# Renewing the normalized input ahead of the value projection, and second parts of every other weight unit by an adding transfer

## The chip, the core and the metric

The kernel runs on one core of a Trainium2 chip. The metric is the device time of one execution in microseconds (us), the median of several. TensorE (PE) does the matrix products, VectorE (DVE) and ScalarE (ACT) the elementwise work, GpSimd (POOL) a few small operations and a part of the transfers, and SyncE (SP) issues the others.

## What is computed

The reference is a trunk of two layers over 512 tokens of width 1024. A layer normalizes its input, projects it, runs three mixers beside each other (a recurrence, A; latent attention, B; forgetting attention, C), merges them with sigmoid gates that are made from the same normalized input, and then runs a feed-forward part and a per-layer input part.

```
for i in range(DEPTH):                        # DEPTH = 2
    h = rmsnorm(x, mix_norm[i])
    z = h @ w_in[i]
    u_rnn, u_gelu, c_q, ckv_rope, fq, fk, fv, f_logit, gate_logit = split_columns(z)
    y_a = rglru_branch(u_rnn, u_gelu, ...) @ w_br_a[i]      # conv, gates, scan over the tokens
    y_b = mla_branch(c_q, ckv_rope, ...) @ w_br_b[i]
    y_c = fox_branch(fq, fk, fv, f_logit, ...) @ w_br_c[i]  # softmax, causal, forget bias
    g = sigmoid(gate_logit + gate_b[i])                     # three gates of width 1024
    merged = g[0] * y_a + g[1] * y_b + g[2] * y_c
    x = x + merged @ w_o[i]
    x = x + swiglu(rmsnorm(x, ffn_norm[i]))
    x = x + sigmoid(rmsnorm(x, ple_norm[i]) @ w_ple_gate[i]) * (p[i] @ w_ple[i])
return rmsnorm(x, final_norm)
```

## The kernel before

Every activation lies as pages of 128 channels x 512 tokens, eight pages for width 1024. To keep float32 accuracy each factor of a product is held in two parts: a high part, rounded by a cast, and a low part, which is the value less its high part. One 128x128 tile of weights times one page is then three matmuls of 128x512 (`mm3`): high by high, high by low, low by high. A page of two parts lies in the pool `pr` (31 pages), a plain page in `pf` (20 pages).

The weights are one stream of 606 units of 128x512 (four 128x128 tiles each, so twelve matmuls a unit), in the order in which the program uses them. SP loads a unit into one of 4 buffers `raw`. `Stream._split` makes the parts: ACT casts the high part (L112) and DVE subtracts it from the loaded unit (L113), into one of 8 buffers `hl`. A unit's buffer comes free when the last of its matmuls has run, and then the unit that comes eight later can be split into it.

In a layer's mixing stage (`mix`) the first projections use pages `X`, which are x times the gain without the division by the norm, since the norm isn't known yet; each result is multiplied by the row of reciprocal norms `r` afterwards (`scaled`, one DVE instruction each, 128x512). Later projections use `Xn`, the input normalized in full. `renorm` makes page k of it: a DMA in POOL's queue loads x again from DRAM (L695, from `xT` in layer 0 and from the scratch `xs` in layer 1) into a `pf` page, DVE multiplies by gain and `r` (a scalar_tensor_tensor with `vec`), ACT casts the high part, DVE subtracts for the low part. `drop_x` gives the pages `X` and `r` back.

The order in question is this. After the gates of the recurrence come `lru_tail` (ACT square roots; then for each of four channel groups a multiply-add, a product, a scan over the tokens at L666, a product with the GELU branch, and the split into `yA`), the value projection of mixer C (`values`, units 24 to 31 in layer 0), and then `attention`, which sets score and probability products among a plan of other projections: key projection 1 (`fp(1, 0)`, units 32 and 33), the merge of channel group 0 (`mg(0, 0)`, its gate of units 34 and 35, and its product with `yA`), the gate of group 1 (`mg(0, 1)`), query projection 1 (`fp(1, 1)`) and so on. In the kernel before, the first three of these use `X` and `r`; the eight renewals stand in the plan between them, in three portions, and `fp(1, 1)` is the first to need `Xn`. No line orders engines directly: a scheduler lists the instructions of each engine from the program's order, its priorities (the splitting of weights has a high one) and its own estimates, and that list then stands.

Of the kernel before, what the change touches and what calls it, by code (L numbers as in the profile page):

```python
# [10 lines left out]
F32 = mybir.dt.float32  # L11
F32R = mybir.dt.float32r
I32 = mybir.dt.int32
AF = mybir.ActivationFunctionType
ALU = mybir.AluOpType
# [3 lines left out]
KD = D // 128  # L19
# [18 lines left out]

NUNITS = 606
KEPT = NUNITS - 16  # L40
PACKED = (8, 9, 311, 312)


# [41 lines left out]
class Stream:  # L85
# [15 lines left out]
    def _split(self, u):  # L101
        s = (u % self.nraw) * 512
        src = self.raw[:, s:s + 512]
        if u >= KEPT:
            self.kept[u] = self.pages.take()
        hi, lo = self._parts(u)
        if u in PACKED:
            hi, lo = (x.rearrange("p (k c) -> p k c", c=128)[:, :, 64 * i:64 * i + 64]
                      for i, x in ((0, hi), (1, hi)))
            src = src.rearrange("p (k c) -> p k c", c=128)[:, :, 0:64]  # L110
        with self.tc.high_priority():
            self.nc.scalar.copy(hi, src)  # L112
            self.nc.vector.tensor_tensor(lo, src, hi.bitcast(F32), op=ALU.subtract)  # L113

    def _parts(self, u, c=slice(0, 512)):
        if u in self.kept:
# [5 lines left out]
    def _ensure(self, u):  # L122
        last = min(u + self.nhl - 1, max(u + 4, KEPT - 1), NUNITS - 1)
        while self.loaded < min(self.nraw, NUNITS):
            self._load(self.loaded)
            self.loaded += 1
        while self.done <= last:
            self._split(self.done)
            self.done += 1
            while self.loaded < min(self.done + self.nraw, NUNITS):  # L130
                self._load(self.loaded)
                self.loaded += 1
# [34 lines left out]
class Trunk:  # L167
# [273 lines left out]
    def mix(self, layer):  # L441
        nc = self.nc
        L, st, X = layer, self.st, self.xp
# [42 lines left out]
        rT = self.cols(NT)  # L486
# [24 lines left out]
        def key_and_forget():  # L511
# [3 lines left out]
            for k, x in enumerate(X):  # L515
                assert self.w.pos // 4 in PACKED
                wh, _ = self.w.tile(("kf", L, k))
# [84 lines left out]
        def fox_proj(p, X, r):  # L602
            return [
                self.dense(self.win(L, C_FK + 128 * p), X, ev_heads(kp, p, r, True, False)),
                self.dense(self.win(L, C_FQ + 128 * p), X, ev_heads(qp, p, r, True, True)),
            ]

        def values(spec, X, rT):

            V = []  # L610
            bs = [self.banks.take() for _ in range(NT)]
            for k, x in enumerate(X):
                wh, wl = self.w.wide(spec + (k,))
                for j in range(NT):
                    c = slice(j * 128, (j + 1) * 128)
                    self.mm3(bs[j][:, :], x.h[:, c], x.l[:, c], wh, wl, k == 0, k == len(X) - 1)
                    yield
            for j in range(NT):
                g = pr.take()
                V.append(g)  # L620
                dst = g.ap.rearrange("p (h t d) -> p h t d", h=HEADS, t=2)
                src = bs[j].rearrange("p (h d) -> p h d", h=HEADS)
                hi = dst[:, :, 0, :]
                if rT is None:
                    self.split(hi, dst[:, :, 1, :], src)
                else:
                    r = rT[:, j:j + 1]
                    self.act(hi, src, AF.Copy, scale=r)
                    self.stt(dst[:, :, 1, :], src, r, hi.bitcast(F32), ALU.mult, ALU.subtract)
                self.banks.give(bs[j])  # L630
            self.V = V


        yA = [None] * 4
# [20 lines left out]
        def lru_tail():  # L655

            with ExitStack() as after:
                for i in last_tanh:
                    after.enter_context(self.tc.issue_after(i.ins))
                for q in tT:  # L660
                    self.act(q.ap, q.ap, AF.Sqrt, bias=self.eps[:, 1:2])
            for t in range(4):
                a, bb, q = aT[t], bT[t], tT[t]
                self.stt(q.ap, a.ap, 1.0, q.ap, ALU.add, ALU.mult)
                self.tt(bb.ap, bb.ap, q.ap)
                nc.vector.tensor_tensor_scan(q.ap, a.ap, bb.ap, 0.0, op0=ALU.mult, op1=ALU.add)  # L666
                self.stt(q.ap, q.ap, 0.25, gx[t].ap, ALU.mult, ALU.mult)
                yA[t] = pr.take()
                self.split(yA[t].h, yA[t].l, q.ap)
                for p in (q, a, bb, gx[t]):  # L670
                    p.free()
# [13 lines left out]
            p.free()  # L685

        lru_tail()
        self.run(values(("fv", L), X, rT))
        Xn = [None] * KD

        def renorm(*ks):

            for k in ks:
                t, p = pf.take(), pr.take()
                nc.gpsimd.dma_start(t.ap, x_dram[k])  # L695
                self.stt(t.ap, t.ap, self.v(L, V_MIX + k), st["r"].ap, ALU.mult, ALU.mult)
                self.split(p.h, p.l, t.ap)
                t.free()
                Xn[k] = p
            return  # L700
            yield

        def drop_x():
            for p in X:
                p.free()
            st.pop("r").free()
            return
            yield


        merged = [None] * KD
        out_pages = [None] * KD
# [32 lines left out]
        def merge(n, j, ys, X=Xn, r=None):  # L745
            box = []
            yield from gate(n, j, box, X, r)
            yield from branch(n, j, ys, box)
# [154 lines left out]
        def fp(p, w, X=Xn, r=None):  # L903
            return (fox_proj(p, X, r)[w], 8)

        def mg(n, j, ys, X=Xn, r=None):
            return (merge(n, j, ys, X, r), 12)
# [56 lines left out]
        def done_c():  # L964
            for p in oC:
# [5 lines left out]
        lkv = [(latent(ckv, skv, C_CKV, j), 8) for j in range(2)]  # L971
        tail = chain(gate(2, 2, boxes[2, 2]), gate(2, 3, boxes[2, 3]))
        attention(True, oC, [
            [fp(1, 0, X, st["r"]), (renorm(0, 1), 0), mg(0, 0, yA, X, st["r"]), (renorm(2, 3, 4), 0),
             mg(0, 1, yA, X, st["r"]), (renorm(5, 6, 7), 0), (drop_x(), 0), fp(1, 1), mg(0, 2, yA)],
            [fp(2, 0), mg(0, 3, yA), mg(0, 4, yA), fp(2, 1), mg(0, 5, yA)],
            [fp(3, 0), mg(0, 6, yA), fp(3, 1)] + lq,
            lkv + [mg(0, 7, yA), (free_yA(), 0), (latent_sums(), 0), gt(2, 0), (latent_norm(), 0),
# [160 lines left out]
    def ple_last(self, X, pw):  # L1139

        L, st = DEPTH - 1, self.st
        self.w.align()
        assert self.w.pos == 4 * KEPT
        fin = [{}, {}]
        half = [slice(0, SEQ // 2), slice(SEQ // 2, SEQ)]

        def part(i, j):
            t = half[i]
            b = self.banks.take()
            for k in range(KD):  # L1150
                if i == 0:
                    wh, wl = self.w.tile(("w_ple_gate", L, 128 * j, 128, k))
                else:
                    wh, wl = self.w.again(4 * KEPT + KD * j + k)
                self.mm3(b[:, :SEQ // 2], wh, wl, X[k].h[:, t], X[k].l[:, t], k == 0, k == KD - 1)
# [236 lines left out]
```

## Time and profile before

| | us |
|---|---|
| median of 3 runs | 1833.01 (1832.89 to 1834.19) |
| profiled execution | 1832.69 |
| its span on the core | 1830.8 |
| PE busy | 1805.4 |
| DVE busy | 1210.4 |
| ACT busy | 817.5 |
| POOL busy | 117.2 |

The span is what the trace covers, from first to last instruction; the 1.9 us between it and the execution's time lie around it. Busy times of engines run beside each other and don't add up. In the views below a group's row gives the number of instructions, the busy time of all and the mean of one in ns; in brackets or behind an arrow stands what ended an engine's idle time.

### The profile page before, as it was taken

Reading aid. Unit: us, or ns where it says so; the run is one execution under the profiler, and the core shown is the slowest. Engines: PE = TensorE matmul, PEld = TensorE weight load, DVE = VectorE, ACT = ScalarE, POOL = GpSimd, SP = SyncE. Lnnn points to the kernel's source line nnn. Section 1 sums busy time; section 2 is a strip of 40 time slices with the busy share of each in tenths; the row PEclk is TensorE's granted clock in tenths of the full one; section 3 lists DMA queues with packets and bytes.
Section 4 is the critical chain, followed back from the end, with each engine's and each line's share of the span. In section 5 each row is a group of like instructions: output and inputs, shape, how many; then the busy total and the mean of one; then the engine's idle time right before and its main releaser. Section 6 shows DMA issues by size and latency. Waiting matters only on the chain.

```text
span 1830.8 us, 24152 instructions
## 1 busy us (share of the span) xinstructions
PE 1805.4 (99%) x8476; PEld 1504.4 (82%) x8476; DVE 1210.4 (66%) x2421; ACT 817.5 (45%) x1562; POOL 117.2 (6%) x234
## 2 busy tenths in 40 slices
PE   9979999999999999999999899999999999999997
PEld 7858888888888888888888788888888888888887
DVE  8896678866665555444778966888576655553446
ACT  5755556553333333223448556565533333332243
POOL 1130001100000000000102200010000000000000
PEclk9989999999999999999999999999999999999999
DMA  6232223324322332322433322243242332233331
GB/s 205 88 117 81 82 81 116 97 71 133 98 93 97 98 98 97 108 95 98 132 111 116 105 85 78 89 121 88 81 131 94 98 97 94 97 110 98 98 98 47
DMA packets 98825, 184.17 MB, mean 101 GB/s; under 512 B 13552, under 2 KB 14752, under 8 KB 98704
## 3 DMA queue, kind: packets, MB, share of 16 engines
q1 hardware_dynamic: 89280, 162.04, 27.1%
q0 software_dynamic: 8416, 19.45, 3.9%
q8 instruction: 66, 1.08, 0.2%
q10 hardware_dynamic: 1008, 1.14, 0.2%
q14 instruction: 55, 0.45, 0.1%
HBM read 173.98 MB, written 4.21 MB: 97 GB/s over the span
## 4 chain that ended last, share of the span: by engine, by line
PE 95%; DVE 3%; ACT 1%; issue 1%; DVEq 0%; ACTq 0%
PE bank L237 93%; PE bank L830 2%; DVE pf L218 1%; DVE pr L221 1%; ACT pf L230 0%; DVE hl L113 0%; DVE pf L666 0%; ACT pr L566 0%; DVE pf L221 0%; DVE pr L218 0%; ACT hl L112 0%; DVE small L838 0%; DVE bank L221 0%; DVE small L218 0%; ACT L230 0%
## 5 line engine op out<-in xcount | busy, mean ns | idle before, releaser
L237 PE MATMUL bank<-pr,hl 128*128 128x512 f32 (+1 forms) x6812 | 1605.2, 392 | 10.6 <-DVE pr L221 5.5
L237 PEld LDWEIGHTS bank<-pr,hl 128*128 128x128 f32 (+1 forms) x6812 | 1269.7, 188 | 274.5 <-DVE pr L221 8.0
L112 ACT CAST hl<-raw 128x512 fp32r<-128x512 f32 x590 | 364.2, 618 | 654.0 <-PE bank L237 438.8
L113 DVE TENSOR_TENSOR hl<-raw,hl 128x512 fp32r<-128x512 f32 x590 | 404.6, 686 | 365.4 <-ACT hl L112 349.5
L221 DVE TENSOR_TENSOR pf<-pf 128x512 f32<-128x512 f32 (+3 forms) x235 | 151.2, 652 | 31.9 <-ACT pf L230 29.8
L221 DVE TENSOR_TENSOR pf<-bank,pf 128x512 f32<-128x512 f32 (+3 forms) x198 | 132.9, 676 | 56.8 <-PE bank L237 31.7
L230 ACT ACTIVATE pf<-pf 128x512 f32<-128x512 f32 (+1 forms) x145 | 86.0, 600 | 112.5 <-DVE pf L221 109.8
L237 PE MATMUL bank<-pr 128*128 128x256 f32 (+4 forms) x704 | 119.6, 301 | 4.1 <-ACT pf L230 4.1
L237 PEld LDWEIGHTS bank<-pr 128*128 128x128 f32 (+1 forms) x704 | 103.9, 191 | 14.5 <-ACT pf L230 4.4
L230 ACT ACTIVATE pf<-bank,small 128x128 f32<-128x128 f32 (+3 forms) x130 | 69.0, 532 | 45.8 <-DVE small L838 42.8
L221 DVE TENSOR_TENSOR pr<-pf,pr 128x512 fp32r<-128x512 f32 (+3 forms) x126 | 85.6, 683 | 4.7 <-ACT pr L233 3.1
L855 ACT CAST pth<-bank 128x128 fp32r<-128x128 f32 (+3 forms) x128 | 54.2, 426 | 69.7 <-PE bank L830 65.6
L233 ACT CAST pr<-pf 128x512 fp32r<-128x512 f32 (+2 forms) x114 | 70.3, 620 | 29.0 <-DVE pf L218 19.2
L838 DVE TENSOR_REDUCE small<-bank 128x1 f32<-128x128 f32 (+3 forms) x128 | 61.7, 485 | 19.2 <-PE bank L237 18.2
L221 DVE TENSOR_TENSOR ptl<-bank,pth 128x128 fp32r<-128x128 f32 (+3 forms) x128 | 61.7, 484 | 13.8 <-ACT pth L855 11.7
L237 PE MATMUL bank<-hl,pr 128*128 128x512 f32 x240 | 56.5, 390 | 0.0
L830 PE MATMUL bank<-identr,pf 128*128 128x128 f32 x320 | 55.4, 274 | 0.0
L237 PEld LDWEIGHTS bank<-hl,pr 128*128 128x128 f32 x240 | 44.9, 188 | 9.2
L225 DVE TENSOR_SCALAR pf<-pf,small 128x128 f32<-128x128 f32 (+3 forms) x128 | 48.3, 383 | 2.6
L218 DVE SCALAR_TENSOR_TENSOR pf<-pf,bank 128x512 f32<-128x512 f32 x48 | 32.7, 684 | 23.7 <-PE bank L237 23.3
L230 ACT ACTIVATE pf<-bank,vec 128x512 f32<-128x512 f32 x60 | 40.9, 689 | 15.1 <-PE bank L237 14.7
L830 PEld LDWEIGHTS bank<-identr,pf 128*128 128x128 f32 x320 | 39.8, 141 | 7.2
(112 smaller groups left out, 793.2 us busy)
## 6 DMA issues: line engine op xcount, KB each, us to landing
raw<-wst SPq DMA_DIRECT2D x606, 256.0 KB, 2.6
pf<-xT POOLq DMA_DIRECT2D x16, 256.0 KB, 3.1
pr<-pr POOLq DMA_DIRECT2D x32, 128.0 KB, 2.5
pf<-xs POOLq DMA_DIRECT2D x16, 256.0 KB, 3.1
pf<-trig POOLq DMA_DIRECT2D x12, 256.0 KB, 3.1
pf<-xT SPq DMA_DIRECT2D x8, 256.0 KB, 5.4
xs<-pf POOLq DMA_DIRECT2D x8, 256.0 KB, 2.8
pf<-pT POOLq DMA_DIRECT2D x4, 256.0 KB, 3.1
```

Source lines behind the costliest of these rows:

```text
L112: self.nc.scalar.copy(hi, src)
L113: self.nc.vector.tensor_tensor(lo, src, hi.bitcast(F32), op=ALU.subtract)
L218: self.nc.vector.scalar_tensor_tensor(out, a, s, b, op0=op0, op1=op1)
L221: self.nc.vector.tensor_tensor(out, a, b, op=op)
L225: self.nc.vector.tensor_scalar(out, a, s1, None, op0=op0)
L230: return self.nc.scalar.activation(out, a, f, **kw)
L233: self.nc.scalar.copy(hi, src)
L237: self.nc.tensor.matmul(out, a, b, start=start, stop=stop, skip_group_check=True)
L830: nc.tensor.transpose(T[:, c], p2.ap[:, c], self.ident[:, :])
L838: nc.vector.reduce_max(R[t][:, 0:1], S[:, :m], axis=AX.X, negate=True)
L855: self.nc.scalar.copy(hi, src)
```

## The change

The set `ADDED` has the odd units 11 to 129 and 315 to 433, which is 120 units, in the mixing stage of each layer. For these the low part isn't made by DVE: ACT writes the negated high part into the low part's place (a second ACT instruction, 128x512), and a DMA in POOL's queue adds the unit from DRAM to it. The load of the unit into `raw` stays, as the high part is cast from it.

The eight renewals stand ahead of the value projection in the program's order and `drop_x` behind it, so the plan has none of them, and `fp(1, 0)`, `mg(0, 0)` and `mg(0, 1)` use `Xn`. The three multiplications by `r` after these fall away in each layer.

```diff
+ADDED = {*range(11, 130, 2), *range(315, 434, 2)}
...
         with self.tc.high_priority():
             self.nc.scalar.copy(hi, src)
-            self.nc.vector.tensor_tensor(lo, src, hi.bitcast(F32), op=ALU.subtract)
+            if u in ADDED:
+
+                self.nc.scalar.activation(lo, hi.bitcast(F32), AF.Copy, scale=-1.0)
+                c = 512 * (u % 2)
+                self.nc.gpsimd.dma_start(lo, self.wdram[u // 2][:, c:c + 512], accum_op=ALU.add)
+            else:
+                self.nc.vector.tensor_tensor(lo, src, hi.bitcast(F32), op=ALU.subtract)
...
         lru_tail()
-        self.run(values(("fv", L), X, rT))
...
+        renorm(*range(KD))
+        self.run(values(("fv", L), X, rT))
+        drop_x()
...
         attention(True, oC, [
-            [fp(1, 0, X, st["r"]), (renorm(0, 1), 0), mg(0, 0, yA, X, st["r"]), (renorm(2, 3, 4), 0),
-             mg(0, 1, yA, X, st["r"]), (renorm(5, 6, 7), 0), (drop_x(), 0), fp(1, 1), mg(0, 2, yA)],
+            [fp(1, 0), mg(0, 0, yA), mg(0, 1, yA), fp(1, 1), mg(0, 2, yA)],
```

**On PE.** These are PE's rows of before in layer 0, from the last of the value products on. Products with `pr,hl` are projections: bank_68 is key projection 1, bank_70 the gate of group 0, bank_72 the gate of group 1, bank_67 the product with `yA`; products with `pr` alone are scores, the x2 of 128x512 those of the last block of queries.

```order
L237 MATMUL bank_72<-hl,pr 128x512 x3
L237 MATMUL bank_73<-pr 128x128
L237 MATMUL bank_68<-pr,hl 128x512 x21
L237 MATMUL bank_69<-pr 128x256
L237 MATMUL bank_68<-pr,hl 128x512 x3
L237 MATMUL bank_70<-pr,hl 128x512 x18
L237 MATMUL bank_73<-pr 128x128
L237 MATMUL bank_69<-pr 128x256
L237 MATMUL bank_71<-pr 128x384 x2
L237 MATMUL bank_70<-pr,hl 128x512 x6
L237 MATMUL bank_67<-pr,hl 128x512
L237 MATMUL bank_72<-pr,hl 128x512 x22
```

And these of the changed kernel, from the last score products on, with the same banks. What the dots leave out are transposes of probabilities.

```order
L245 MATMUL bank_67<-pr,hl 128x512
L245 MATMUL bank_73<-pr 128x512 x2
L245 MATMUL bank_68<-pr,hl 128x512 x5
L245 MATMUL bank_70<-pr,hl 128x512 x5
L245 MATMUL bank_72<-pr,hl 128x512 x5
L245 MATMUL bank_67<-pr,hl 128x512 x5
...
L245 MATMUL bank_68<-pr,hl 128x512
L245 MATMUL bank_70<-pr,hl 128x512
L245 MATMUL bank_72<-pr,hl 128x512
...
L245 MATMUL bank_68<-pr,hl 128x512 x14
L245 MATMUL bank_70<-pr,hl 128x512 x14
L245 MATMUL bank_72<-pr,hl 128x512 x14
```

Before, each of the three projections runs in one go ahead of the last scores; now the three stand side by side, a few matmuls of each at a time, and 14 of the 24 of each stand behind the last scores and the transposes.

**On DVE.** These are DVE's rows of before in layer 0 where the recurrence begins to be finished; L537 is the scan of the forget gates, L666 that of the recurrence, L113 a weight unit's low part.

```order
L537 SCALAR_TENSOR_TENSOR pf<-one,pf 8x512
L218 SCALAR_TENSOR_TENSOR pf<-pf 128x512 x2
L113 TENSOR_TENSOR hl<-raw,hl 128x512
L221 TENSOR_TENSOR pf<-pf 128x512 x2
L218 SCALAR_TENSOR_TENSOR pf<-pf 128x512 x2
L113 TENSOR_TENSOR hl<-raw,hl 128x512
L666 SCALAR_TENSOR_TENSOR pf<-pf 128x512
L221 TENSOR_TENSOR pr<-pf,pr 8x512
L666 SCALAR_TENSOR_TENSOR pf<-pf 128x512
```

And the same place of the changed kernel, and after the dots the end of it, some 50 rows on; a row with `pf,vec` is the multiplication of a renewal, and `pr<-pf,pr 128x512` a low part (of a renewed page or of `yA`).

```order
L226 SCALAR_TENSOR_TENSOR pf<-pf,vec 128x512
L121 TENSOR_TENSOR hl<-raw,hl 128x512
L545 SCALAR_TENSOR_TENSOR pf<-one,pf 8x512
L226 SCALAR_TENSOR_TENSOR pf<-pf 128x512 x2
L229 TENSOR_TENSOR pf<-pf 128x512 x2
L674 SCALAR_TENSOR_TENSOR pf<-pf 128x512
L229 TENSOR_TENSOR pr<-pf,pr 128x512
...
L226 SCALAR_TENSOR_TENSOR pf<-pf,vec 128x512
L850 RECIPROCAL small<-small 128x1
L226 SCALAR_TENSOR_TENSOR pf<-pf,vec 128x512
L233 TENSOR_SCALAR pf<-pf,small 128x512
L229 TENSOR_TENSOR pr<-pf,pr 128x512 x2
```

One renewal now has its multiplication ahead of the scan of the forget gates; the other seven stand among the work of the recurrence and the values, in the order of pages 2, 4, 5, 6, 1, 3, 7, and the two rows behind the dots with `vec` are pages 3 and 7, behind most of the softmax of the score blocks.

**On POOL.** These are POOL's rows of before in layer 0 at the end of the forget gates' chain (L378, L379), and the DMA to which it leads (L534), for which the scan L537 waits.

```order
L378 TENSOR_SCALAR pf<-pf 128x32
L379 TENSOR_TENSOR pf<-pf 128x32
L378 TENSOR_SCALAR pf<-pf 128x32
L379 TENSOR_TENSOR pf<-pf 128x32
L534 DMA pf<-pf 8x16x32
L695 DMA pf<-xT 128x512
L589 DMA pr<-pr 2x1x512 x6
```

And the same place of the changed kernel; L119 is an adding transfer, L702 the load of a renewal, L595 a memset of 4 partitions.

```order
L595 MEMSET pr 4x512
L387 TENSOR_TENSOR pf<-pf 128x32
L386 TENSOR_SCALAR pf<-pf 128x32
L387 TENSOR_TENSOR pf<-pf 128x32
L386 TENSOR_SCALAR pf<-pf 128x32
L702 DMA pf<-xT 128x512
L595 MEMSET pr 4x512
L387 TENSOR_TENSOR pf<-pf 128x32
L595 MEMSET pr 4x512
L542 DMA pf<-pf 8x16x32
L119 DMA hl<-wst 128x512
L702 DMA pf<-xT 128x512
```

Memsets and the first renewal's load have moved into the chain, ahead of its DMA, and adding transfers stand between the loads of the renewals behind it.

## Rows read from the trace of the kernel before

**Rows 1.** The page: busy time and share of each engine.

```profile
PE 1805.4 (99%) x8476; PEld 1504.4 (82%) x8476; DVE 1210.4 (66%) x2421; ACT 817.5 (45%) x1562; POOL 117.2 (6%) x234
```

**Rows 2.** Layer 0's stretches: us; busy PE, PEld, DVE, ACT, POOL; clock, DMA.

```profile
60.00:80.00 20.00, 20.00 (x90) 16.54 (x90) 18.25 (x33) 17.47 (x30) 2.99 (x7) 1.00 0.25 84
80.00:100.00 20.00, 20.00 (x91) 16.56 (x90) 15.02 (x23) 16.46 (x27) 7.95 (x17) 1.00 0.32 106
90.50:127.50 37.00, 26.99 (x107) 19.87 (x105) 36.81 (x64) 22.09 (x40) 15.32 (x30) 0.86 0.41 130
117.00:130.00 13.00, 7.83 (x15) 4.61 (x16) 12.94 (x28) 7.84 (x17) 2.85 (x6) 0.50 0.28 86
130.60:150.00 19.40, 19.40 (x100) 16.42 (x99) 15.02 (x36) 11.63 (x26) 1.94 (x4) 1.00 0.23 75
```

**Rows 3.** The same view, for layer 1.

```profile
993.00:1027.00 34.00, 29.46 (x130) 23.56 (x128) 33.68 (x56) 22.92 (x41) 12.25 (x24) 0.97 0.45 140
1025.00:1031.40 6.40, 4.89 (x12) 3.33 (x11) 6.34 (x13) 2.35 (x6) 0.88 (x2) 0.50 0.32 99
1031.70:1050.00 18.30, 18.30 (x94) 15.36 (x93) 15.08 (x39) 11.45 (x27) 0.49 (x2) 1.00 0.27 84
```

**Rows 4.** PE in order of time: start, us, idle before; last stalls of both layers.

```profile
127.48 1.22 PE L237 MATMUL bank<-pr,hl 128*128 128x512 f32 x2 [1.39 <-DVE pr L221]
1027.13 1.22 PE L237 MATMUL bank<-pr,hl 128*128 128x512 f32 x2 [1.51 <-DVE pr L221]
```

**Rows 5.** DVE's groups by form, 90.5 to 127.5 us.

```profile
L113 DVE TENSOR_TENSOR hl<-raw,hl 128x512 fp32r<-128x512 f32 x10 | 6.8, 682 | 0.0
L221 DVE TENSOR_TENSOR pr<-pf,pr 128x512 fp32r<-128x512 f32 x10 | 6.7, 680 | 0.0
L218 DVE SCALAR_TENSOR_TENSOR pf<-pf 128x512 f32<-128x512 f32 x8 | 5.3, 683 | 0.0
L218 DVE SCALAR_TENSOR_TENSOR pf<-pf,vec 128x512 f32<-128x512 f32 x7 | 5.2, 739 | 0.0
L666 DVE TENSOR_TENSOR_SCAN pf<-pf 128x512 f32<-128x512 f32 x4 | 4.9, 1218 | 0.0
L218 DVE SCALAR_TENSOR_TENSOR pr<-bank,small,pr 128x512 fp32r<-128x512 f32 x4 | 2.9, 743 | 0.0
L221 DVE TENSOR_TENSOR pf<-pf 128x512 f32<-128x512 f32 x4 | 2.6, 682 | 0.0
L221 DVE TENSOR_TENSOR pf<-bank,pf 128x512 f32<-128x512 f32 x3 | 2.0, 675 | 0.0
L221 DVE TENSOR_TENSOR bank<-bank,fmask 128x128 f32<-128x128 f32 x5 | 1.3, 288 | 0.0
L838 DVE TENSOR_REDUCE small<-bank 128x1 f32<-128x256 f32 x1 | 0.4, 418 | 0.0
```

**Rows 6.** DVE in order of time: the forget gates' scan, and the recurrence's start in both layers.

```profile
89.26 1.22 DVE L537 TENSOR_TENSOR_SCAN pf<-one,pf 8x512 f32<-8x512 f32 x1 [3.03 <-DMA pf<-pf]
90.50 1.29 DVE L218 SCALAR_TENSOR_TENSOR pf<-pf 128x512 f32<-128x512 f32 x2
993.23 1.31 DVE L218 SCALAR_TENSOR_TENSOR pf<-pf 128x512 f32<-128x512 f32 x2 [1.34 <-ACT pf L230]
```

**Rows 7.** POOL in order of time: first and last of the chain in layer 0.

```profile
76.46 0.31 POOL L376 TENSOR_SCALAR pf<-pf 128x32 f32<-128x32 f32 x1 [30.66 <-DVE pf L221]
86.27 0.72 POOL L534 DMA_DIRECT2D pf<-pf  x1 [1.10 <-ACT pf L230]
```

**Rows 8.** POOL's groups, 90 to 130 us.

```profile
L695 POOL DMA_DIRECT2D pf<-xT x8 | 4.5, 560 | 19.8 <-issue 10.1 <-PE bank L237 6.7 <-DVE pr L221 2.9
L587 POOL MEMSET pr<- 4x512 f32 x8 | 4.0, 518 | 0.7 <-PE bank L237 0.7
```

**Rows 9.** The page: ACT's cast of a unit, and two kinds of transfer to their landing.

```profile
L112 ACT CAST hl<-raw 128x512 fp32r<-128x512 f32 x590 | 364.2, 618 | 654.0 <-PE bank L237 438.8
...
pf<-xT POOLq DMA_DIRECT2D x16, 256.0 KB, 3.1
pf<-xT SPq DMA_DIRECT2D x8, 256.0 KB, 5.4
```

More of the change, by code (lines that the diff above doesn't have):

```diff
@@ L699, in renorm @@
                 Xn[k] = p
-            return
-            yield
         def drop_x():
@@ L706, in drop_x @@
             st.pop("r").free()
-            return
-            yield
+        renorm(*range(KD))
+        self.run(values(("fv", L), X, rT))
+        drop_x()
         merged = [None] * KD
```

## The prediction

> **What bounds the kernel now.** I read the busy times first: PE has 1805.4 of 1830.8 us, DVE 66% and ACT 45% [rows 1]. So the time is PE's work plus the little that it stands still or runs slow, and a change to the other engines counts only where PE waits for them. Next I went through stretches of 20 us. Away from the two ends PE stands still in one place of each layer: it has 26.99 of 37.0 us from 90.5 to 127.5 [rows 2], and 29.46 of 34.0 from 993 to 1027 [rows 3]. That is 10.0 and 4.5 us, with DVE at 36.81 of 37.0 and 33.68 of 34.0 beside it: there DVE is the bound. It is where the recurrence is finished, the values are evicted, the normalized input is renewed and the first scores go through the softmax. In order of time, PE's last stall ends at 127.48 and at 1027.13, each released by DVE's low part of a page [rows 4]. Behind these stalls the granted clock is 0.50 (1.2 of 2.4 GHz) until about 130.5 and 1031.5, and 1.00 from 130.6 and 1031.7 on [rows 2, 3]. PE goes on dense there, so half of (130.5 - 127.48) and of (1031.5 - 1027.13), 1.5 and 2.2 us, is lost to the clock. All that can be won here is 10.0 + 4.5 + 3.7 = 18.2 us.
>
> A matmul of 128x512 takes PE 20.00 / 90 = 0.222 us at full clock [rows 2], and a unit, twelve of them, 2.67 us.
>
> **The adding transfers.** They take 120 x 0.682 us = 82 us of subtractions off DVE [rows 5]. I count nothing for it behind the two stalls: PE is at 19.40 of 19.40 and 18.30 of 18.30 there [rows 2, 3], and a lighter DVE releases nobody earlier. What they add must then be hidden. ACT's negation is an operation on 128x512 like its cast, 0.62 us [rows 9]; 20 us hold 7.5 units, so some four negations, 2.3 us, against 2.5 and 3.5 us that ACT has left in 60 to 80 and 80 to 100 [rows 2]. Just covered; without the cover the square roots, and all behind them, come later by what is missing. The trace has no adding transfer. The nearest rows are a plain one of the same size in the same queue, 3.1 us to its landing, and the slowest of this size, 5.4 us [rows 9]; I take 3.1 to 5.4, nearer to the first, whose queue it shares. With cast, negation and 0.56 us of issue [rows 8] a unit's low part is there 4.9 to 7.2 us after its buffer came free. That buffer is free seven units ahead, 18.7 us, and where several projections run side by side some 54 matmuls ahead by the order of PE, 12 us. Hidden by 5 us or more.
>
> In POOL's queue the adds stand among the renewals' loads, which wait for free pages; the adds of units 33, 35 and 37 wait with them. All three are ahead of page 1's load, so PE, which needs page 1 to go far in these units, has them in time.
>
> **The move.** Before, the key projection and the first two gates used `X`, which lies there from the start. They and the product with `yA` are 24 + 24 + 24 + 12 matmuls, and with two of the next accumulations 86 of them had run when PE's last stall of layer 0 ended at 127.48. They were what PE did while DVE was busy. Now the first three need renewed pages, in the order 0 to 7. By PE's order only 19 stand ahead of the last scores, then 20 that need pages 1 and 2, then the page 3 group and the rest.
>
> When do the pages come? DVE starts on the recurrence at 90.50, just behind the scan of the forget gates [rows 6]. From there to page 3's low part DVE's order has 57 instructions: 2 subtractions of units (0.682), 7 multiplications of renewals (0.739) and 7 low parts (0.680), 8 multiply-adds (0.683), 4 products (0.682), 4 scans (1.218), 4 low parts of `yA` and one of the forget gates (0.680), 4 values (0.743), 4 reductions (0.418) and 12 short ones (masks, reciprocals, scalings), which I take at the 0.288 of a mask. The sum is 35.9 us [rows 5]. Busy times overlap a little, as an instruction begins before the one ahead has drained: in this stretch all groups add to 41.5 us in 37.0, a factor of 0.89. So page 3 comes 32.1 us after 90.5, at 122.6, and page 1, eleven and more rows earlier, by the same addition after 26.8 us, at 117.3.
>
> PE starts again at 117.3 with 86 - 19 = 67 matmuls to catch up on, 14.9 us. It has stood still for long and so gets half clock first; with the 3.0 us of before that costs 1.5 us. By then the 20 are done at 123.2, so page 3 (122.6) costs no second wait. PE is at the point of 127.48 at 117.3 + 14.9 + 1.5 = 133.7; before it was there at 127.48 + 1.5 = 129.0 in undisturbed terms. **Layer 0: +4.7 us**, up to +6 if the clock stays low longer while the 20 run.
>
> In layer 1 DVE starts at 993.23, behind the square roots [rows 6]; up to three more ACT operations (two negations, one cast of a renewed page) stand ahead of these, of which I count one, 0.6 us. Here one renewal more is ahead, and to page 3's low part DVE has 51 instructions: 3 subtractions, 7 multiplications, 10 low parts, 4 scans, 8 multiply-adds, 4 products, 4 values and 11 short ones, 33.3 us by the same rows, 29.7 with the factor. Page 3 comes at 1023.5. PE has then done 42, since pages 0 to 2 are ready earlier; before it had done 85 at 1027.13. It needs 43 x 0.222 = 9.5 us more, to 1033.0, against 1027.13 + 2.2 = 1029.3. **Layer 1: +3.7 us**, and 1.5 more if this wait too brings half clock; I take +4.3.
>
> What the change saves inside these stretches is in the sums: eight subtractions fewer (10 to 2) in layer 0 and the three multiplications by `r` (0.675) fewer [rows 5]. DVE's last page comes 5 us earlier than before's last stall; but PE has had far less to do until then.
>
> **The sum.** 4.7 + 4.3 = +9.0 us on the profiled 1832.69, which is 0.3 below the median: **1842 us** for the median. A measurement of this kernel can tell about 0.2%, 3.7 us, from no change.
>
> **Rivals.**
>
> *Faster: the renewal fits in ahead of the crowded stretch.* DVE has 15.02 of 20 us in 80 to 100 and stands still for 3.03 us ahead of the scan [rows 2, 6]; a renewal takes 1.4 us, so three could go there. If the recurrence itself begins earlier by as much as 5 us in each layer (85.5 and 989), or that much of the work is ahead of it, the sum above comes to zero; from there on each us is won twice, once a layer. With 8 us earlier in both, 1842 - 16 = 1826. The floor is 1832.7 - 18.2 = 1814.5. For it: DVE loses some 3.4 us of subtractions ahead of the chain. Against it: the order puts only one (layer 0) or two (layer 1) renewals ahead, and the start hangs on POOL's chain and on the square roots, not on DVE. 0.11.
>
> *No change: the lighter DVE starts both stretches earlier.* POOL's chain of the forget gates waits for DVE at 76.46 [rows 7], and five subtractions, 3.4 us, are gone ahead of it. If all of it reaches the recurrence's start in both layers, the loss is 9.0 - 6.8 = 2.2 us: 1835. Against it: POOL's order now has four memsets (0.52) and a load's issue (0.56) [rows 8] in that chain, 2.6 us, and in layer 1 the square roots decide. 0.14.
>
> *Much slower: the adds land late.* From the point where cast, negation, issue and landing take over 18.7 us, the ring of 8 buffers turns slower than PE: 30 turns over 240 units, each longer by the excess. A landing of 20 us gives 30 x (21.8 - 18.7) = 93 us: 1935. For it: nothing here shows what an add into the on-chip memory costs. Against it: the rows for plain transfers are four times shorter, and POOL issues its loads in 0.56 us with DVE busy for 36.81 of 37.0 us beside it [rows 2, 8]. 0.05. The Trainium skill ("SBUF — State Buffer", § Who interferes with whom) says that GpSimd and DVE share a pair of ports, that a DVE instruction in a two-port mode locks GpSimd out, and that a transfer which GpSimd describes itself then stalls; by that rule the adds would be the first to suffer. The trace doesn't bear it out in this stretch, as the 0.56 us shows.
>
> **Chances.** The forecast 0.70, as I trust the order for what PE lacks, and only its sizes are open; faster 0.11, no change 0.14, much slower 0.05. Slower by over 0.2% is the first and the last: 0.75. The forecast's own range is 1837 to 1849 (the losses at 2 and 2.5 us a layer, or at 8 each). The range from 1832 to 1850 takes in the case of no change and leaves out about 0.18.
>
> **What would show it.** In PE's order of time: after the last value products a long idle time, well over the 4 us of before, ended by DVE's low part of a page at 117 to 118 in layer 0; half clock behind it; the dense stretch going on to the next scores 4 to 6 us later than before, and 3 to 5 us in layer 1. In DVE's order of time: the recurrence at 89.5 to 91 and page 3's low part at 121 to 124. In the stretches behind: PE full, DVE lighter by 82 us in all, and the adds landing in 3 to 6 us. I'd be wrong if the recurrence began 5 us earlier, if DVE's list took its rows in less than 27 us, if the adds landed in over 10 us, or if PE stood still in a stretch that is dense now.

## The result, and the profile after

The changed kernel takes 1843.09 us in the median (1842.6 to 1843.43, 4 runs), beside 1833.6 (1832.89 to 1834.66, 4 runs) of the kernel before: a ratio of 1.0051, interval 1.0034 to 1.0068, or 9.4 us more by this ratio (9.5 by the two medians). 1842 was forecast.

This is the profile's page of the changed kernel, its span and its busy times:

```profile
span 1841.7 us, 24278 instructions
PE 1809.9 (98%) x8476; PEld 1508.0 (82%) x8476; DVE 1140.5 (62%) x2295; ACT 880.0 (48%) x1682; POOL 220.7 (12%) x354
```

PE runs the same 8476 matmuls as before [rows 1], so the span can be split in two. What lies outside PE's busy time is its idle time: 1841.7 - 1809.9 = 31.8 us now, 1830.8 - 1805.4 = 25.4 before, 6.4 more. The busy time of the same matmuls grows by 4.5 us, as they take longer each where the granted clock is half. DVE is lighter by 70 us (82 were forecast), and the kernel is slower.

Where it was lost is seen from an event that comes at the end of each layer, the load of the per-layer input (`pT`, in POOL's queue). One line each of the view by source line, before and after; the two times are the first and the last start, which lie in layer 0 and in layer 1:

```profile
L1085 POOL DMA_DIRECT2D pf<-pT x4: 536/538/538, 735.6 to 1641.0; - x4
```

```profile
L1090 POOL DMA_DIRECT2D pf<-pT x4: 536/537/538, 741.9 to 1652.0; - x4
```

Layer 0 ends 741.9 - 735.6 = 6.3 us later, and layer 1 adds 11.0 - 6.3 = 4.7 us.

PE of the changed kernel in order of time, with its stalls in both layers:

```profile
103.51 0.69 PE L245 MATMUL bank<-pr 128*128 128x384 f32 x1 [8.38 <-DVE pr L226]
...
113.30 2.07 PE L245 MATMUL bank<-pr,hl 128*128 128x512 f32 x4 [2.93 <-ACT pr L241]
116.27 1.22 PE L245 MATMUL bank<-pr 128*128 128x512 f32 x2 [0.90 <-ACT pf L238]
117.29 7.05 PE L245 MATMUL bank<-pr,hl 128*128 128x512 f32 x20
...
1015.07 1.22 PE L245 MATMUL bank<-pr,hl 128*128 128x512 f32 x2 [7.53 <-ACT pr L241]
...
1018.27 8.66 PE L245 MATMUL bank<-pr,hl 128*128 128x512 f32 x26 [0.48 <-DVE pr L226]
...
1027.23 2.91 PE L245 MATMUL bank<-pr,hl 128*128 128x512 f32 x12
```

PE runs dry at 95, in the middle of what was dense work before, and at 1007.5. The 8.38 us end with DVE's second part of a value page (L226), which gives back the bank that the next scores take, the next stalls with parts of renewed pages (L241) and with the softmax (L238). The 20 matmuls that follow at 117.29 take 7.05 us, 0.35 each. In layer 1 the 26 from 1018.27 on take 8.66 us, 0.33 each.

DVE of the changed kernel in order of time: in layer 0 the start of the recurrence, three low parts of which one is page 1's, and those of pages 3 and 7; in layer 1 the start and the low part of page 3.

```profile
89.22 1.29 DVE L226 SCALAR_TENSOR_TENSOR pf<-pf 128x512 f32<-128x512 f32 x2
...
114.69 1.90 DVE L229 TENSOR_TENSOR pr<-pf,pr 128x512 fp32r<-128x512 f32 x3
...
121.18 1.29 DVE L229 TENSOR_TENSOR pr<-pf,pr 128x512 fp32r<-128x512 f32 x2
...
999.49 0.69 DVE L226 SCALAR_TENSOR_TENSOR pf<-pf 128x512 f32<-128x512 f32 x1 [2.06 <-ACT pf L238]
...
1028.03 0.68 DVE L229 TENSOR_TENSOR pr<-pf,pr 128x512 fp32r<-128x512 f32 x1
```

And its stretches (us, busy PE, PEld, DVE, ACT, POOL, clock, DMA share, GB/s):

```profile
90.50:127.50 37.00, 23.92 (x81) 17.43 (x80) 33.18 (x62) 19.96 (x39) 14.60 (x27) 0.68 0.47 119
100.00:116.50 16.50, 8.29 (x18) 5.04 (x19) 16.50 (x30) 5.98 (x12) 7.94 (x15) 0.50 0.49 129
117.00:130.00 13.00, 13.00 (x53) 10.54 (x52) 7.49 (x17) 5.13 (x13) 1.05 (x2) 0.80 0.06 20
130.60:150.00 19.40, 19.40 (x93) 16.16 (x92) 11.04 (x24) 14.84 (x31) 4.50 (x5) 1.00 0.79 187
1007.60:1015.00 7.40, 0.00 (x0) 0.00 (x0) 7.40 (x13) 2.84 (x7) 3.81 (x8) 0.64 1.04 258
```

In the stretch of 37 us PE runs 81 matmuls and transposes where it ran 107 [rows 2]. From 100 to 116.5 the clock is half already, and DVE has no idle time. It has none in layer 1's stall either (7.40 of 7.40 us). There the DMA engines are full too (share 1.04), and ACT waits for the load of a weight unit ahead of the cast of the page for which PE waits:

```profile
1013.31 0.62 ACT L114 CAST hl<-raw 128x512 fp32r<-128x512 f32 x1 [4.56 <-DMA raw<-wst]
...
1014.41 1.13 ACT L241 CAST pr<-pf 128x512 fp32r<-128x512 f32 x2
```

So the end of PE's 7.53 us, at 1015.07, isn't set by DVE alone. PE's long run of matmuls begins at 1018.27, behind DVE again; what the late load costs, no run took apart.

### The profile page after: what moved, and what is told of

It reads as the page before. It is cut to its first block, busy times and chain, and to the rows that moved or that the text cites. A ratio compares the mean times of both kernels' runs of the same rounds, so it can differ in the third digit from the quotient of the medians.

```text
span 1841.7 us, 24278 instructions
## 1 busy us (share of the span) xinstructions
PE 1809.9 (98%) x8476; PEld 1508.0 (82%) x8476; DVE 1140.5 (62%) x2295; ACT 880.0 (48%) x1682; POOL 220.7 (12%) x354
## 4 chain that ended last, share of the span: by engine, by line
PE 95%; DVE 2%; ACT 1%; DMA 1%; issue 1%; POOL 0%; DVEq 0%; POOLq 0%; ACTq 0%
PE bank L245 93%; PE bank L836 2%; ACT pf L238 1%; DVE pf L226 1%; DMA pf<-xs 0%; DMA hl<-wst 0%; DVE pf L674 0%; DVE pr L229 0%; DVE pf L229 0%; DMA pf<-xT 0%; POOL pf L386 0%; POOL pf L387 0%; DVE pr L226 0%; ACT hl L114 0%; DVE hl L121 0%
## 5 line engine op out<-in xcount | busy, mean ns | idle before, releaser
L121 DVE TENSOR_TENSOR hl<-raw,hl 128x512 fp32r<-128x512 f32 (+1 forms) x470 | 322.7, 687 | 362.3 <-ACT hl L114 347.9
L229 DVE TENSOR_TENSOR pf<-bank,pf 128x512 f32<-128x512 f32 (+3 forms) x192 | 128.9, 677 | 65.5 <-PE bank L245 33.4
L119 POOL DMA_DIRECT2D hl<-wst x120 | 105.3, 883 | 493.6 <-ACT hl L117 396.3
L238 ACT ACTIVATE pf<-pf 128x512 f32<-128x512 f32 (+1 forms) x145 | 85.7, 600 | 112.7 <-DVE pf L229 110.3
L245 PE MATMUL bank<-pr 128*128 128x256 f32 (+5 forms) x704 | 121.4, 304 | 9.8 <-DVE pr L226 8.4
L245 PEld LDWEIGHTS bank<-pr 128*128 128x128 f32 (+2 forms) x704 | 104.7, 192 | 21.4 <-DVE pr L226 8.8
L229 DVE TENSOR_TENSOR pr<-pf,pr 128x512 fp32r<-128x512 f32 (+2 forms) x122 | 82.5, 684 | 7.3 <-ACT pr L241 6.2
L238 ACT ACTIVATE pf<-bank,small 128x512 f32<-128x512 f32 (+3 forms) x130 | 68.8, 531 | 36.0 <-DVE small L844 32.6
L241 ACT CAST pr<-pf 128x512 fp32r<-128x512 f32 (+1 forms) x114 | 69.9, 618 | 29.1 <-DVE pf L226 18.5
L117 ACT ACTIVATE hl<-hl 128x512 fp32r<-128x512 f32 x120 | 75.5, 631 | 2.0
```

The source lines that it names most:

```text
L117: self.nc.scalar.activation(lo, hi.bitcast(F32), AF.Copy, scale=-1.0)
L119: self.nc.gpsimd.dma_start(lo, self.wdram[u // 2][:, c:c + 512], accum_op=ALU.add)
L229: self.nc.vector.tensor_tensor(out, a, b, op=op)
L238: return self.nc.scalar.activation(out, a, f, **kw)
L245: self.nc.tensor.matmul(out, a, b, start=start, stop=stop, skip_group_check=True)
```

## The experiments

The theory: PE lost the 72 matmuls of a layer that needed no renewed page, and they were its work while DVE was busy; the adding transfers neither give nor cost much. Rivals: the adds cost, through late transfers; or the early renewals cost, through their own DVE and POOL work. All medians are of five runs or more, and each ratio is against runs of the kernel before on the same chip. A difference from before is worked out from this ratio; between two other kernels I subtract the medians, and by the ratios these differences come out the same within 0.6 us.

**The two halves apart.** The first kernel has the move and no adds:

```diff
-ADDED = {*range(11, 130, 2), *range(315, 434, 2)}
+ADDED = set()
```

> The move without any adding transfer (the set of added units is empty). If the loss is PE's lack of projections while DVE is busy, it stays: 1840 to 1846 us, PE's longest stalls in both layers 7 to 9 us as with the whole change, and as DVE has two or three more subtractions to do before the last page, 1 to 3 us more than the whole change at most. Rival, that the adding transfers make the loss (POOL's queue and the DMA engines late with the renewals' loads): 1831 to 1835 us.

Measured: 1845.43 us, ratio 1.0061 (1.0049 to 1.0074). The move alone has the whole loss, 11.2 us. Its stalls aren't those that I expected: PE stands still more often and for less, in these stretches 3.59 us at the longest and not 7 to 9, and ahead of the recurrence in layer 0 DVE waits 3.05 us for a renewal's load, where it waits 1.03 in the whole change. The second has the adds in the kernel before, and nothing else:

> The adding transfers of the change, with the renewals and the plan as before. If the loss is the move's, nothing is lost: 1826 to 1833 us, where a gain comes from four to six subtractions fewer (3 to 4 us of DVE a layer) in the two stretches in which DVE bounds PE, and none elsewhere. Rival, that the adding transfers make the loss: 1838 to 1843 us.

Measured: 1820.8 us, ratio 0.9926 (0.9913 to 0.994), 13.5 us faster. Not only don't the adds cost; they give more than the 1 to 8 us that I allowed them. The third is the whole change, but the three projections use `X` and `r` as before, and `drop_x` stands in the plan behind them:

```diff
-            [fp(1, 0), mg(0, 0, yA), mg(0, 1, yA), fp(1, 1), mg(0, 2, yA)],
+            [fp(1, 0, X, st["r"]), mg(0, 0, yA, X, st["r"]), mg(0, 1, yA, X, st["r"]),
+             (drop_x(), 0), fp(1, 1), mg(0, 2, yA)],
```

> The whole change, but the key projection and the first two gates still use the unnormalized pages and the multiplication afterwards; the old pages are given back behind them. So the renewals stand early and the adds are there, only PE has its 72 matmuls free of the renewals again. If the lack of these is the cause, the loss is gone: 1826 to 1834 us and no stall over 5 us. Rival, that the early renewals themselves (their loads in POOL's queue, their DVE work ahead of the recurrence) make the loss: 1838 to 1843 us.

Measured: 1821.43 us, ratio 0.9932 (0.9919 to 0.9944). That is the time of the adds alone. So the renewals' early place costs 0.6 us or nothing, and the use of `Xn` in three projections makes all the difference between 1821.4 and 1843.1: 21.7 us. The profile's pages show it in PE's idle and busy time. These are the span and the busy times of the adds alone (the third kernel has 1819.0 and PE 1802.4):

```profile
span 1819.0 us, 24284 instructions
PE 1802.3 (99%) x8476; PEld 1502.7 (83%) x8476; DVE 1140.3 (63%) x2301; ACT 881.0 (48%) x1682; POOL 222.1 (12%) x354
```

Idle 16.7 us against 25.4 before, 8.7 fewer, and 3.1 us less of busy time for the same matmuls; together the 11.8 of the spans. DVE's busy time, 1140, is that of the whole change. The same lightening of DVE gives 11.8 us in one place and hides in a loss of 10.9 in the other.

**How much PE's missing work explains.** One of the three projections, the key projection, gets `X` back (`drop_x` stands behind it):

```diff
-            [fp(1, 0), mg(0, 0, yA), mg(0, 1, yA), fp(1, 1), mg(0, 2, yA)],
+            [fp(1, 0, X, st["r"]), (drop_x(), 0), mg(0, 0, yA), mg(0, 1, yA), fp(1, 1), mg(0, 2, yA)],
```

> The whole change, but the key projection still uses the unnormalized pages, and the two gates the renewed ones: 24 of the 72 matmuls are free of the renewals again in each layer. If PE's lack of work is the loss, 24 x 0.222 = 5.3 us a layer come back: 1830 to 1835 us, a little under half of the way from 1843 to the 1821 with all three kept. Rival, that one projection waiting is enough to hold up PE (it fills its queue in order): 1840 to 1844 us.

Measured: 1837.34 us, ratio 1.0019 (1.001 to 1.0028). It is faster than the whole change by 5.8 us, about half of what the 24 matmuls would make up, and lies between the two ranges. The direction holds and the size doesn't. Its stalls are there still, in layer 0 (of its slowest execution, 1839.53, which is the profiled one):

```profile
101.94 0.82 PE L245 MATMUL bank<-pr 68*128 68x128 f32 x4 [2.56 <-DMA pr<-pr]
105.76 3.07 PE L245 MATMUL bank<-pr,hl 128*128 128x512 f32 x6 [2.99 <-DVE pr L226]
...
112.95 0.89 PE L245 MATMUL bank<-pr,hl 128*128 128x512 f32 x2 [2.62 <-ACT pr L241]
115.98 1.22 PE L245 MATMUL bank<-pr 128*128 128x512 f32 x2 [2.15 <-ACT pf L238]
117.65 7.14 PE L245 MATMUL bank<-pr,hl 128*128 128x512 f32 x18 [0.45 <-DVE pr L229]
```

PE starts again at 117.65, no earlier than 117.29, and at half clock again. A projection that runs gives DVE work as well: its multiplication by `r`, its head splits, and one more subtraction for the weights that it lets through.

Then the order of the pages. The kernel has the whole change, and the three projections take the renewed pages in the order in which DVE finishes them.

```diff
+ORDERS = ((0, 2, 4, 5, 6, 1, 3, 7), (2, 1, 0, 4, 5, 6, 3, 7))
...
-        for k, x in enumerate(xs):
+        for i, k in enumerate(getattr(xs, "order", range(n))):
+            x = xs[k]
...
-            self.mm3(b[:m], wh[:, :m], wl[:, :m], x.h, x.l, k == 0, k == n - 1)
+            self.mm3(b[:m], wh[:, :m], wl[:, :m], x.h, x.l, i == 0, i == n - 1)
```

> The whole change, but the key projection and the first two gates take the renewed pages in the order in which DVE finishes them (0, 2, 4, 5, 6, 1, 3, 7 in layer 0, and 2, 1, 0, 4, 5, 6, 3, 7 in layer 1) in place of 0 to 7; DVE's list is the same, row for row. If the loss is that these 72 matmuls come after the late pages 1 and 3, PE has all but the last two pages' 18 done when page 3 comes, 30 matmuls fewer to catch up in layer 0 and 25 in layer 1, and stands at half clock for less: 1826 to 1833 us. Rival, that PE is held by the softmax of the scores or by having to wait for renewed pages at all, in whatever order: 1839 to 1844 us.

Measured: 1838.94 us (1835.42 to 1840.45), ratio 1.0026 (1.0015 to 1.0038): 4.2 us back, at the edge of the rival's range and well short of mine. The profiled execution is the fastest of them, 1835.42, so it shows a part of where the rest went and not its size in the median. The first row below is the PE stretch that starts with the pages at hand; the others are stalls further on that the whole change doesn't have there.

```profile
106.61 11.28 PE L250 MATMUL bank<-pr,hl 128*128 128x512 f32 x41
...
147.25 0.63 PE L844 MATMUL bank<-identr,pf 128*128 128x128 f32 x4 [1.85 <-ACT pf L243]
150.12 0.63 PE L250 MATMUL bank<-pr 128*128 128x384 f32 x2 [0.95 <-ACT pf L243]
152.07 0.50 PE L250 MATMUL bank<-pr 128*128 128x256 f32 x2 [1.32 <-DVE pr L231]
153.12 5.06 PE L250 MATMUL bank<-pr,hl 128*128 128x512 f32 x21 [0.54 <-DVE ptl L234]
```

PE has 41 matmuls to run from 106.61 on where it stood still, and then it comes to the next transposes and scores before ACT and DVE are through with the softmax ahead of them: the four stalls take 4.7 us. In layer 1 there is no such place. By the loads of `pT` this layer takes 1644.0 - 739.0 = 905.0 us, and 905.4 before:

```profile
L1098 POOL DMA_DIRECT2D pf<-pT x4: 536/536/538, 739.0 to 1644.0; - x4
```

DVE's list isn't the same row for row, as I had put it. In layer 0 two subtractions of weight units at 116.30 and a third at 121.32 now stand ahead of page 3's low part, which is there at 124.3 and not at 121.8:

```profile
116.30 1.30 DVE L126 TENSOR_TENSOR hl<-raw,hl 128x512 fp32r<-128x512 f32 x2
...
123.65 0.68 DVE L234 TENSOR_TENSOR pr<-pf,pr 128x512 fp32r<-128x512 f32 x1
```

So the order of the pages and what comes with it are worth 4.2 of the 21.7 us. The order by itself isn't shown, and why the executions of this one spread over 5 us stays open.

**Where the adds gain.** Four kernels with the renewals and the plan of before, and adds in one place only, are told by their set of units. All units from 28 to 50 and 332 to 354:

> Renewals and plan as before, and adding transfers for every unit from 28 to 50 and from 332 to 354, and for no other: DVE loses all its subtractions in the two stretches that it bounds, 7 us in each, and none elsewhere. If DVE's work in these stretches is what PE waits for, each us of DVE is up to one of PE: 1821 to 1829 us. Rival, that PE's stall hangs on the softmax chain and the renewals' loads and not on DVE's amount of work: 1831 to 1835 us. Second rival, that adding transfers of units in a row land late: over 1836 us.

Measured: 1826.86 us, ratio 0.9957 (0.9945 to 0.997), 7.9 us and within the range. Only behind the stretches (odd units 51 to 129 and 355 to 433):

> Renewals and plan as before; adding transfers only for the odd units 51 to 129 and 355 to 433, 80 of the 120, which lie behind the two stretches. If a lighter DVE is worth nothing where PE is full, and the adds themselves cost nothing: 1832 to 1835.5 us. Rival, that the gain of the adds alone comes from these units too (a part of the slack carried along, fewer small waits): 1824 to 1830 us. Rival, that they cost: over 1837 us.

Measured: 1834.53 us, ratio 1.0004 (0.9995 to 1.0013): nothing. Only ahead (odd units 11 to 23, 315 to 327):

> Renewals and plan as before; adding transfers only for the odd units 11 to 23 and 315 to 327, seven a layer, whose subtractions lie ahead of the recurrence's start. If the gain of the adds alone comes from an earlier start (the scan of the forget gates at 84.6 us in place of 89.3), this has most of it: 1823 to 1828 us. Rival, that the start hangs on other work and only the subtractions inside the stretches count: 1832 to 1835 us.

Measured: 1830.23 us, ratio 0.9982 (0.9973 to 0.9991): 3.3 us, between the two ranges. Only within (odd units 25 to 49, 329 to 353):

> Renewals and plan as before; adding transfers only for the odd units 25 to 49 and 329 to 353, thirteen a layer, whose subtractions lie in or just ahead of the stretches that DVE bounds. If what counts is DVE's sum inside (four to five subtractions, 3 us a layer, and some half clock): 1825 to 1830 us. If only the earlier start counts: 1832 to 1835 us.

Measured: 1824.48 us, ratio 0.995 (0.9938 to 0.9963): 9.2 us, half a us better than the range. These thirteen don't only lighten the stretch; they bring its start forward as well. The scan of the forget gates begins at 89.26 us before [rows 6] and at 84.61 with all the adds. This is its row with the units ahead, and then with those within:

```profile
88.46 1.22 DVE L544 TENSOR_TENSOR_SCAN pf<-one,pf 8x512 f32<-8x512 f32 x1 [0.67 <-DMA pf<-pf]
```

```profile
86.43 1.22 DVE L544 TENSOR_TENSOR_SCAN pf<-one,pf 8x512 f32<-8x512 f32 x1 [2.91 <-DMA pf<-pf]
```

So an earlier start and a lighter stretch aren't told apart by the two sets of units. Ahead and within add to 12.5, and a kernel with just these forty units has them all:

> Renewals and plan as before; adding transfers for the odd units 11 to 49 and 315 to 353, and no others: the denser kernel without its four even units a layer, and the adds alone without those behind. If the units behind are worth nothing, it is at the 1820.8 of the adds alone, 1819 to 1823 us, and it was the four even units that cost 5 us. Rival, that the missing units behind cost the denser kernel its gain: 1824 to 1828 us.

Measured: 1819.69 us, ratio 0.9923 (0.991 to 0.9935), 14.1 us ahead of before, the lowest median of all, though not told apart from the adds alone. More adds among them make it worse. With four even units more in each layer:

> Renewals and plan as before; adding transfers for the odd units 11 to 49 and 315 to 353 and for four even ones among them in each layer (30, 34, 38, 42 and 334, 338, 342, 346), none behind. If the gains ahead of the stretches and within add up (4 and 10 us) and the units behind are worth nothing, at least the 1820.8 of the adds alone, and the four even ones give up to 2.7 us a layer more: 1815 to 1821 us. Rival, that more adds in a row are late, as the DMA engines are full (share 0.99 with every unit added): 1823 to 1828 us.

Measured: 1826.1 us, ratio 0.9961 (0.9949 to 0.9974): the time is in the rival's range, and as the forty units without these are at 1819.69, it is the eight even ones that cost 6.4 us. From 85 to 130 us its adds take 7.2 us to land as a median, 5.9 with the forty. But no stall of PE over 0.2 us ends with an add's landing in this kernel's two stretches. What differs in layer 0 is the start. These are the recurrence's first rows with the forty units, and then with the even ones:

```profile
87.75 1.31 DVE L225 SCALAR_TENSOR_TENSOR pf<-pf 128x512 f32<-128x512 f32 x2 [0.86 <-ACT pf L237]
```

```profile
89.19 1.31 DVE L225 SCALAR_TENSOR_TENSOR pf<-pf 128x512 f32<-128x512 f32 x2 [2.36 <-ACT pf L237]
```

DVE waits there for ACT's square roots, and between 60 and 88.4 us ACT has five negations ahead of them in place of three, 3.1 us for 1.9. That is the term of the prediction that has the square roots come later by what isn't covered. How much of the 6.4 us it is, and how much the late transfers are, stays open. In the kernel with every unit of the two stretches added the transfers fill the DMA engines in both stretches (us, busy PE, PEld, DVE, ACT, POOL, clock, DMA share, GB/s):

```profile
90.50:127.50 37.00, 31.20 (x124) 24.12 (x124) 34.49 (x66) 33.12 (x63) 25.24 (x43) 0.91 0.99 242
993.00:1027.00 34.00, 29.34 (x131) 23.22 (x130) 32.33 (x60) 30.03 (x60) 23.56 (x38) 1.00 1.05 262
```

And two short stalls of PE in layer 1 (0.27 and 0.53 us) end with an add's landing:

```profile
1003.53 3.02 PE L244 MATMUL bank<-pr,hl 128*128 128x512 f32 x12 [0.27 <-DMA hl<-wst]
1007.42 4.87 PE L244 MATMUL bank<-pr,hl 128*128 128x512 f32 x20 [0.53 <-DMA hl<-wst]
```

With ten odd units more at the start and ahead of layer 1 (3, 5, 7, 299 to 309, 313), on top of all of the adds alone:

> The adds alone, and three more odd units at the start (3, 5, 7) and seven ahead of layer 1's mixing stage (299 to 309, 313). If every subtraction ahead of the recurrence brings its start forward, two layers gain up to 2 us each: 1816 to 1820 us. Rival, that the start hangs on the square roots and POOL's chain by then, or that more adds crowd the transfers at the kernel's start: 1820 to 1824 us.

Measured: 1821.8 us, ratio 0.9935 (0.9922 to 0.9949): no gain, as the rival had it. The scan of the forget gates begins at 81.77 there, 2.8 us ahead of the adds alone, but DVE then waits 2.57 us for ACT's square roots, and the recurrence begins at 88.28, behind the 87.41 of the adds alone.

## Why the prediction was right, and which of its steps were not

**What bounds the kernel, and that PE lacks work.** Shown. The three projections on renewed pages make the loss (21.7 us between the third experiment and the whole change), and neither the adds nor the place of the renewals does by itself. That the loss goes by the number of matmuls is not shown: a third of them returned brings 5.8 us. And one of the signs of being wrong came: PE stood still from 95.1 us on, where it was dense before (20.00 of 20.00 from 80 to 100, [rows 2]). I had looked for the long idle time at its end, at 117 to 118; it ended at 103.51, with a value page.

**The start and DVE's list** were sized well. In layer 0 the recurrence began at 89.22 and not at 90.50 [rows 6], and page 3's low part came at 121.18 + 0.6 = 121.8, where 122.6 was forecast; the list took 32.6 us, forecast 32.1. In layer 1 it ran from 999.49 to 1028.7, 29.2 us against 29.7; less the 6.3 us that layer 0 was late it began at 993.2, as before [rows 6].

**PE's second start** was at 117.29, forecast 117.3, and that is luck. The forecast has PE wait for page 1 until then. Page 1's low part is one of the three from 114.69 on, so it was there at 116.6 at the latest; the recurrence had begun 1.3 us earlier than I took. PE stood in the last scores by then, which the softmax let go at 116.27, and the 20 matmuls stood behind these. The wait for the softmax was no term of the sum; it made up for the earlier start.

**The catching up** was sized too low: I let half clock cost 1.5 us, with 3.0 us of it as before [rows 2, 4]. The 20 matmuls took 7.05 us in place of 4.4, so 2.6 us were lost, and ten transposes came between. In layer 1 the forecast has PE wait for page 3 with 42 matmuls done. That step failed: when page 3's low part came at 1028.7 (1022.4 without layer 0's 6.3 us, forecast 1023.5), PE had begun 37 of the 42 and went on without a stall. It was held by its late start, at 1015.07 and 1018.27, and by half clock behind that: the 26 matmuls took 8.66 us in place of 5.8. Layer 0 lost 6.3 for 4.7, layer 1 4.7 for 4.3; 11.0 in the profile, 9.4 by the ratio, for 9.0. The mechanism is right, PE's lack of work while DVE is busy; that the sum came so near is in part luck.

**The adds.** "A lighter DVE releases nobody earlier" behind the stalls: shown by the kernel with adds only there. They landed in 4.2 us as a median, in the 3.1 to 5.4 that I took. But the sum hid how much DVE's relief is worth ahead and inside. I counted the "eight subtractions fewer (10 to 2)" as the change's saving. These are the subtractions of weight units in DVE's groups from 88 to 122 us, in the move without adds and in the whole change:

```profile
L121 DVE TENSOR_TENSOR hl<-raw,hl 128x512 fp32r<-128x512 f32 x5 | 3.4, 682 | 0.0
```

```profile
L121 DVE TENSOR_TENSOR hl<-raw,hl 128x512 fp32r<-128x512 f32 x2 | 1.4, 688 | 0.0
```

In the same time the kernel before has nine. Four of them are gone without any add: while PE waits for the renewed pages it frees no weight buffer, and the stream stands still. In the move without adds ACT casts no unit between 97.7 and 128.4 us, and that next cast waits for PE. So the adds had little left to take: they bring the moved kernel 2.3 us by the medians (1845.4 to 1843.1), which the two ratios' intervals don't tell from nothing, while alone they bring 13.5. The forecast came out right because it was made on the list of the whole change. Split by its two parts it would have been wrong: it gives the adds alone nothing, and they gain 13.5; and by its eight subtractions (4.9 us with the factor of 0.89, in layer 0) it would have put the move alone well above the whole change, where 2.3 us lie between the two.

**The rival of the earlier start** was right in its mechanism and right in what spoke against it. These are first and last of POOL's chain in the adds alone, and then in the whole change:

```profile
72.75 0.30 POOL L383 TENSOR_SCALAR pf<-pf 128x32 f32<-128x32 f32 x1 [2.70 <-DVE pf L228]
...
81.32 0.72 POOL L541 DMA_DIRECT2D pf<-pf  x1 [0.75 <-DVE pf L225]
```

```profile
73.58 0.30 POOL L384 TENSOR_SCALAR pf<-pf 128x32 f32<-128x32 f32 x1 [2.51 <-DVE pf L229]
...
85.85 0.68 POOL L542 DMA_DIRECT2D pf<-pf  x1 [0.57 <-DVE pf L226]
```

Both begin 3 to 4 us ahead of before [rows 7]. The chain then takes 8.6 us in the one and 12.3 in the other, where the memsets and a renewal's load stand in it. So the chain's DMA comes 5.0 us ahead of before with the adds alone, and in the whole change only 0.4; the recurrence begins 1.3 us ahead there.

**Not told apart:** why one projection returned brings only half of its share. DVE is seen to get more to do, but no run keeps DVE's work as it was and returns the projection.

## What to carry to other kernels

Before an input is made ready "earlier" for work further on, see what that work hides: projections that need nothing are the cover for the stretch in which another engine is the bound, and tying them to that engine's last product cost more here (21.7 us) than the lighter engine saved (13.5). A relief of an engine is worth something in the stretch that this engine bounds and just ahead of it: here 40 of 120 units gave all of the gain, 80 gave nothing, and 8 more set among the 40 took nearly half of it. Measure the parts of a change apart: the +0.5% of the whole are -0.7% by the adds and then +1.2% by the move, while the move alone is +0.6%; the two don't add.

## What the runs showed of the hardware

The page of the changed kernel on transfers (us to their landing), and then the views of the adding line and of the renewals' loads (ns of an issue, least, median and most):

```profile
hl<-wst POOLq DMA_DIRECT2D x120, 256.0 KB, 4.2
pf<-xT POOLq DMA_DIRECT2D x16, 256.0 KB, 4.3
```

```profile
L119 POOL DMA_DIRECT2D hl<-wst x120: 570/877/1204, 27.1 to 1334.9; - x120
```

```profile
L702 POOL DMA_DIRECT2D pf<-xT x8: 547/563/921, 83.2 to 108.7; - x8
```

An adding transfer takes GpSimd 0.88 us to issue (0.57 to 1.2), a plain one of the same size 0.56. It lands 4.2 us after its issue began, as a median, and it makes the plain ones beside it slower: 4.3 us, where they took 3.1 before [rows 9] and 3.1 in the move without adds. The Trainium skill ("DMA: Bandwidth & Descriptors", § Anatomy of one DMA — SWDGE (gpsimd) path) gives a fit of about 2.0 us and the bytes at 436 GB/s for a transfer that GpSimd issues, an estimate of 2.6 us for these 256 KB, with no term for adding. A plain one of before agrees, if its 0.56 us of issue is left out: 2.5 us. An adding one takes 3.3 us without its issue of 0.88; there the measurement is higher, and it decides.
